# A gated linear attention layer rewritten as four phases over all tokens, with the data between them in DRAM

## The chip, the cores and the metric

The kernel runs on one NeuronCore of one Trainium2 chip. The metric is the device time of one execution in microseconds (us); lower is better. The engines have these names in the profile: PE is TensorE (PEld is its weight load), DVE is VectorE, ACT is ScalarE, POOL is GpSimd, and SP is the engine whose queue issues nearly all DMAs.

## The reference

One layer on 2048 tokens of width 1024, all in float32. Cut to what matters here:

```
u    = rmsnorm(h, ln1_g);  proj = u @ w_in                     # q k v g g_lr cb cc cx
o    = rmsnorm(gla(q, k, v, gate), gn_g) * silu(g)             # gated linear attention, chunked
y    = cb * causal_conv3(cc * cx)
h    = h + concat(o, y) @ w_out                                # "mixing"
u2   = rmsnorm(h, ln2_g);  a, b = split(u2 @ w_gate_upffn)     # 1024 -> 2 x 2816   "up"
h    = h + (silu(a) * b) @ w_down                              # 2816 -> 1024       "down"
u3   = rmsnorm(h, ln3_g);  gate = sigmoid(u3 @ w_ple_gate)
h    = h + gate * (p @ w_ple_proj);  out = rmsnorm(h, lnf_g)   # "embed"
```

## The kernel before

Every float32 operand of a long product is split into a high part (a ScalarE cast to a reduced float32) and a low part (a VectorE subtraction), and each product is made in three passes of matmuls (high by high, high by low, low by high; `unit`, line 139). Splits of weights are made by `split` (lines 99 and 100, tiles `hl`), those of activations by `split_into` (lines 149 and 150).

The 2048 tokens are worked on in four blocks of 512, and one block goes through the whole layer before the next one begins: `mixing`, output projection, up, down, embed. The activations of a block never leave the on-chip memory; the weights are loaded and split again for each block. TensorE executes in the order in which the code emits its work (a manual schedule); the other engines and the DMA queue have an order that a scheduler made at build time, and each executes its own list strictly in that order. Small pieces that depend on other engines (transposes, the attention's small products) are put between long products some "ticks" later; a tick is about a dozen matmuls.

The parts of a block that the change touches:

- **Up.** 22 chunks of 128 hidden columns. The first four are plain products (`up`). The other 18 (`up_fast`) use Winograd's form of Strassen's method: the width of 1024 is halved, the two outputs a and b are the two column halves, and the 512 tokens are halved, so that seven products of 256 columns stand for eight. The four sums of weights are made on GpSimd (line 658, 128 columns each), the sums of token operands once per block in `token_sums` (line 633 and the lines behind it).
- **Down.** Plain: for each set of hidden chunks in `DOWN_SETS`, both halves of the output columns, four token tiles, three matmuls of 512 columns per chunk. Sets of down are interleaved with up chunks, so the hidden activations are consumed soon after they are made. The products are added to `h` on VectorE (line 571).
- **Norms.** `norm_to`: a Square with a sum on ScalarE (line 161), two small GpSimd operations (lines 163 and 165), one scaling on VectorE (line 180), eight transposes on TensorE (line 190), and the split.

The rotating buffers of the DMA'd weights (`raw`, 4 buffers) and of their splits (`hl`, 12 buffers) set how far weights can be prepared ahead.

```
for i, n in enumerate(FIRST_ORDER if c == NPLAIN else ORDER):      # up_fast, per hidden chunk
    o, u, bk, hf = PRODUCTS[n]
    unit(half(bk, hf), lhs(o), rhs(*u), 4, lambda: after_product(n), i % 2 == 1)   # 256 columns
...
for n in range(2):                                                 # down, per set
    wd = weights(w_down, [(n * 512, 512)], c0, nch)
    for ti in range(NT):
        unit(ps, lambda k, s: mT[c0 + k][:, s, tok_of(ti)], wd, nch, d_done)       # 512 columns
```

Of the kernel before, what the change touches and what calls it, by code (L numbers as in the profile page):

```python
# [27 lines left out]
DOWN_SETS = ((0, 4), (4, 4), (8, 4), (12, 4), (16, 6))  # L28
GLA_WAIT = 10
N1, N2, N3 = 7, 3, 3  # L30
NPLAIN = 4
ORDER = (1, 2, 4, 5, 6, 7, 3)
FIRST_ORDER = (1, 2, 3, 4, 5, 6, 7)
# [5 lines left out]
def hybrid_layer(ctx: ExitStack, tc: tile.TileContext,  # L39
# [9 lines left out]
    big = ctx.enter_context(tc.tile_pool(name="big", bufs=4))  # L49
    hlp = ctx.enter_context(tc.tile_pool(name="hlp", bufs=12))  # L50
    rawp = ctx.enter_context(tc.tile_pool(name="rawp", bufs=4))
    w4p = ctx.enter_context(tc.tile_pool(name="w4p", bufs=12))
    t2p = ctx.enter_context(tc.tile_pool(name="t2p", bufs=5))
    tiny = ctx.enter_context(tc.tile_pool(name="tiny", bufs=4))
    ps_mm = ctx.enter_context(tc.tile_pool(name="ps_mm", bufs=4, space=bass.MemoryType.PSUM))
    ps_tr = ctx.enter_context(tc.tile_pool(name="ps_tr", bufs=2, space=bass.MemoryType.PSUM))
    ps_g = ctx.enter_context(tc.tile_pool(name="ps_g", bufs=2, space=bass.MemoryType.PSUM))

    def w4(shape, dt=F32):
        return w4p.tile(shape, dt, name="w4")  # L60

    def t2(shape, dt=F32):
        return t2p.tile(shape, dt, name="t2")

    def mm_bank():
        return ps_mm.tile([P, 512], F32, name="mm")

    def tr_bank():
        return ps_tr.tile([P, 512], F32, name="tr")

    def g_bank():
        return ps_g.tile([P, 512], F32, name="g")
# [11 lines left out]
    nc.gpsimd.memset(mhalf, -0.5)  # L84

# [1 line left out]
    def load_pair(src, k0, width, segs):  # L87
        """rows of the k-chunks k0, k0+1 of the named column segments"""
        raw = rawp.tile([P, 2, width], F32, name="raw")
        o = 0  # L90
        for c, n in segs:
            nc.sync.dma_start(out=raw[:, :, o:o + n],
                              in_=src[k0 * P:(k0 + 2) * P, c:c + n].rearrange("(k p) n -> p k n", p=P))
            o += n
        return raw

    def split(raw, width):
        hl = hlp.tile([P, 2, width], F32R, name="hl")
        nc.scalar.copy(out=hl[:, 0, :], in_=raw)  # L99
        nc.vector.tensor_tensor(out=hl[:, 1, :], in0=raw, in1=hl[:, 0, :].bitcast(F32), op=ALU.subtract)  # L100
        return hl
# [25 lines left out]

    def later(n, fn):
        queue.append((clock[0] + n, fn))
        queue.sort(key=lambda e: e[0])  # L130
# [3 lines left out]
    def unit(out_ap, lhs, rhs, nk, done=None, ticks=True):  # L134
        """out = sum over k of lhs(k).T @ rhs(k), three passes over the split operands"""
        n = out_ap.shape[-1]
        for k in range(nk):
            for i, (a, b) in enumerate(PASSES):
                nc.tensor.matmul(out=out_ap, lhsT=lhs(k, a), rhs=rhs(k, b),  # L139
                                 start=(k == 0 and i == 0), stop=(k == nk - 1 and i == 2))  # L140
            if n > 300 and nk > 6 and k == nk // 2 - 1:
                tick()
        if done is not None:
# [8 lines left out]
    def new_uT():  # L152
        return [big.tile([P, 4, 2, T], F32R, name="uT") for _ in range(2)]
# [3 lines left out]

    def rstd_of(src, dst):
        """per-token 1/rms of the [128, 1024] rows of src; dst is overwritten by the squares"""
# [15 lines left out]
    def norm_to(src, u, ti, gain, delay, eng=nc.vector, xn=None):  # L175
        if xn is None:
            xn = w4([P, D])
        rs = rstd_of(src, xn)
        if eng is nc.vector:
            eng.scalar_tensor_tensor(out=xn, in0=src, scalar=rs, in1=gain, op0=ALU.mult, op1=ALU.mult)  # L180
        else:
            nc.vector.tensor_scalar(out=xn, in0=src, scalar1=rs, scalar2=None, op0=ALU.mult)
            eng.tensor_tensor(out=xn, in0=xn, in1=gain, op=ALU.mult)

        def transposes():
            for kk in range(2):
                tp = tr_bank().rearrange("p (a b) -> p a b", b=P)
                for a in range(4):
                    c = (kk * 4 + a) * P
                    nc.tensor.transpose(out=tp[:, a, :], in_=xn[:, c:c + P], identity=ident)  # L190
                split_into(u[kk][:, :, 0, ti * P:(ti + 1) * P], u[kk][:, :, 1, ti * P:(ti + 1) * P], tp)
        if delay is None:
            return transposes
        later(delay, transposes)
# [9 lines left out]
    # remaining constants  # L204
    gng = const.tile([P, 1], F32, name="gng")
    bg = const.tile([P, 2], F32, name="bg")
    cw = const.tile([P, 3, 4], F32, name="cw")
    wgu = const.tile([P, 256], F32, name="wgu")
    lrT = const.tile([P, T], F32, name="lrT")
    smask = const.tile([P, T], F32, name="smask")  # L210
    state = const.tile([P, 2, 256], F32, name="state")
    halo = const.tile([P, 4, 2], F32, name="halo")
    s_sb = {g: const.tile([P, 4, P], F32, name=f"s_sb{g[0]}{g[1]}") for g in GROUPS}
    masks = {L: const.tile([P, 4, P], U8, name=f"mask{L}") for L in LEVELS[2:] + (2,)}

    nc.gpsimd.memset(lrT, 0.0)
    nc.gpsimd.memset(wgu, 0.0)

    def fill_constants():
        after(nc.gpsimd.dma_start(out=wgu[0:16, :], in_=w_gate_up), last["rs"])  # L220
        after(nc.gpsimd.dma_start(out=bg, in_=b_gate.rearrange("(j p) -> p j", p=P), allow_slow_non_contiguous=True), last["rs"])
        after(nc.gpsimd.memset(smask, 1.0), last["rs"])
        nc.gpsimd.memset(smask.rearrange("p (c t) -> p c t", t=P)[:, :, 0:1], 0.0)
        after(nc.gpsimd.dma_start(out=gng, in_=gn_g[0].rearrange("(p o) -> p o", o=1)), last["rs"])
        for i in range(3):
            after(nc.gpsimd.dma_start(out=cw[:, i, :], in_=conv_w[i].rearrange("(j p) -> p j", p=P),
                                      allow_slow_non_contiguous=True), last["rs"])
        after(nc.gpsimd.memset(state, 0.0), last["rs"])
        after(nc.gpsimd.memset(halo, 0.0), last["rs"])
        for t in s_sb.values():  # L230
            after(nc.gpsimd.memset(t, 0.0), last["rs"])

    def fill_mask(L):
        """one where the column's token takes from the row's token at this level"""
        m = masks[L]
        f = t2([P, P])
        after(nc.gpsimd.memset(f, 1.0), last["rs"])
# [616 lines left out]
```

## Time and profile before

| | |
|---|---|
| time, median of 3 runs | 2568.82 us (2568.5 to 2569.72) |
| span of the profiled execution | 2568.4 us |
| PE busy | 2519.0 us (98%) |
| DVE busy | 1706.5 us (66%) |
| ACT busy | 1087.8 us (42%) |
| POOL busy | 918.6 us (36%) |
| DMA | 265.18 MB, mean 103 GB/s |
| mean granted TensorE clock | 0.996 |

The profile is of one execution, whose span is 0.4 us under the median of the times. "Busy" counts the time in which an engine has an instruction in work. A group row reads: line, engine, operation, what is written from what, the shape, the count, then busy time and mean duration in ns of one, then the idle time before it and what ended it. A timeline row reads: start, duration, the merged instructions and their count, and in brackets the idle time before and what ended it. The duration of a TensorE row has a modelled tail, so rates are taken from start to start.

### The profile page before, as it was taken

What the parts mean: (1) busy time and instruction counts of PE and PEld (TensorE: products, weight loads), DVE (VectorE), ACT (ScalarE), POOL (GpSimd) and SP (SyncE); (2) the same over time, 40 slices, a digit from 0 to 9 for tenths busy, and PEclk for the clock granted to TensorE, in tenths of its full rate; (3) what the DMA queues carried; (4) which work ended last, traced back from release to release, by engine and by line L of the source; (5) the groups of instructions that cost most, each with busy time, mean ns of one, the idle gap of its engine ahead of it and who ended that gap; (6) DMA issues with size and microseconds to landing.
All of it is one profiled execution on the core that took longest, in us unless ns stands there. A gap on an engine that the chain in (4) does not pass through costs nothing.

```text
span 2568.4 us, 42117 instructions
## 1 busy us (share of the span) xinstructions
PE 2519.0 (98%) x15616; PEld 2196.1 (86%) x15616; DVE 1706.5 (66%) x2628; ACT 1087.8 (42%) x2104; POOL 918.6 (36%) x1468
## 2 busy tenths in 40 slices
PE   7999999999999999999999999999999999999998
PEld 6778899998878889999887888999878788899987
DVE  4665777776475567777647566777765756677774
ACT  4433444444443344444543343444454334344442
POOL 3301366631130246663121024666313102466620
PEclk9999999999999999999999999999999999999999
DMA  4224233344322333334333223333433232233341
GB/s 157 66 66 132 83 99 99 103 128 149 107 85 69 111 91 99 99 99 154 127 99 99 98 67 91 103 103 99 156 124 108 81 107 72 85 105 102 102 151 52
DMA packets 268686, 265.18 MB, mean 103 GB/s; under 512 B 20656, under 2 KB 202944, under 8 KB 268480
## 3 DMA queue, kind: packets, MB, share of 16 engines
q1 hardware_dynamic: 268288, 262.47, 32.7%
q8 instruction: 122, 2.00, 0.3%
q14 instruction: 84, 0.69, 0.1%
q0 software_dynamic: 192, 0.02, 0.0%
HBM read 254.04 MB, written 8.39 MB: 102 GB/s over the span
## 4 chain that ended last, share of the span: by engine, by line
PE 85%; issue 7%; DVE 4%; POOL 2%; ACT 2%; DMA 0%; SPq 0%; DVEq 0%; POOLq 0%; ACTq 0%
PE mm L139 67%; PE g L139 12%; PE g L330 1%; PE tr L190 1%; DVE uT L150 1%; DVE hl L100 1%; PE g L418 1%; PE g L423 1%; DVE w L281 1%; DVE w L633 1%; POOL rs L165 0%; POOL uT L303 0%; POOL uT L302 0%; PE g L427 0%; PE g L320 0%
## 5 line engine op out<-in xcount | busy, mean ns | idle before, releaser
L139 PE MATMUL mm<-uT,hl 128*128 128x256 f32 (+1 forms) x6528 | 1098.8, 325 | 23.4 <-DVE hl L100 21.8
L139 PEld LDWEIGHTS mm<-uT,hl 128*128 128x128 f32 x6528 | 942.7, 190 | 133.7 <-DVE hl L100 29.6
L100 DVE TENSOR_TENSOR hl<-raw,hl 128x512 fp32r<-128x512 f32 (+2 forms) x1152 | 804.7, 734 | 146.6 <-ACT hl L99 145.1
L99 ACT CAST hl<-raw 128x512 fp32r<-128x512 f32 (+2 forms) x1152 | 634.0, 593 | 618.8 <-PE mm L139 408.7
L658 POOL TENSOR_TENSOR raw<-raw 128x128 f32<-128x128 f32 x1152 | 700.7, 634 | 490.4 <-DMA raw<-in_w_gate_upffn_dram 390.8
L139 PE MATMUL mm<-hl,w 128*128 128x512 f32 x2304 | 542.5, 394 | 0.1
L139 PEld LDWEIGHTS mm<-hl,w 128*128 128x128 f32 x2304 | 430.4, 188 | 100.2 <-ACT w L698 1.8
L139 PE MATMUL mm<-hl,uT 128*128 128x512 f32 (+1 forms) x2256 | 458.0, 361 | 3.4 <-DVE uT L150 2.1
L139 PEld LDWEIGHTS mm<-hl,uT 128*128 128x128 f32 x2256 | 374.8, 188 | 69.1 <-DVE uT L150 2.7
L139 PE MATMUL g<-uT,hl 128*128 128x256 f32 x2592 | 331.4, 282 | 0.0
L139 PEld LDWEIGHTS g<-uT,hl 128*128 128x128 f32 x2592 | 319.6, 189 | 1.7
L571 DVE TENSOR_TENSOR w<-mm,w 128x512 f32<-128x512 f32 x192 | 131.9, 687 | 221.0 <-PE mm L139 200.8
L163 POOL TENSOR_SCALAR ms<-ss 128x1 f32<-128x1 f32 x64 | 19.5, 304 | 652.5 <-ACT w L161 462.9
L149 ACT CAST uT<-tr 128x512 fp32r<-128x512 f32 x96 | 54.0, 583 | 68.8 <-PE tr L190 68.7
L678 DVE TENSOR_TENSOR w<-mm,t 128x256 f32<-128x256 f32 (+1 forms) x144 | 79.3, 553 | 2.3
L698 ACT CAST w<-w 128x512 fp32r<-128x512 f32 x72 | 44.8, 622 | 82.4 <-DVE w L697 82.4
L161 ACT ACTIVATE w<-w 128x1024 f32<-128x1024 f32 x48 | 51.0, 1062 | 56.3 <-DVE w L571 24.0
L150 DVE TENSOR_TENSOR uT<-tr,uT 128x512 fp32r<-128x512 f32 x96 | 63.8, 685 | 10.0 <-ACT uT L149 9.7
L442 POOL TENSOR_SCALAR ms<-ss 128x4 f32<-128x4 f32 x16 | 3.1, 193 | 188.1 <-ACT t L439 188.1
L697 DVE TENSOR_TENSOR w<-w 128x512 f32<-128x512 f32 x72 | 60.1, 835 | 8.3 <-ACT w L696 8.3
L180 DVE SCALAR_TENSOR_TENSOR w<-w,rs,w 128x1024 f32<-128x1024 f32 x32 | 41.1, 1284 | 34.1 <-POOL rs L165 28.8
L149 ACT CAST uT<-w 128x512 fp32r<-128x512 f32 (+1 forms) x32 | 26.8, 837 | 81.7 <-DVE w L554 61.0
(138 smaller groups left out, 1496.4 us busy)
## 6 DMA issues: line engine op xcount, KB each, us to landing
raw<-in_w_gate_upffn_dram SPq DMA_DIRECT2D x576, 128.0 KB, 2.3
raw<-in_w_down_dram SPq DMA_DIRECT2D x88, 512.0 KB, 3.7
raw<-in_w_in_dram SPq DMA_DIRECT2D x64, 512.0 KB, 4.5
w<-in_x_dram SPq DMA_DIRECT2D x32, 512.0 KB, 6.8
raw<-in_w_in_dram SPq DMA_DIRECT2D x64, 256.0 KB, 4.1
raw<-in_w_out_dram SPq DMA_DIRECT2D x32, 512.0 KB, 4.7
raw<-in_w_gate_upffn_dram SPq DMA_DIRECT2D x64, 256.0 KB, 4.1
raw<-in_w_ple_gate_dram SPq DMA_DIRECT2D x32, 512.0 KB, 4.9
```

What stands on the lines that cost most here:

```text
L99: nc.scalar.copy(out=hl[:, 0, :], in_=raw)
L100: nc.vector.tensor_tensor(out=hl[:, 1, :], in0=raw, in1=hl[:, 0, :].bitcast(F32), op=ALU.subtract)
L139: nc.tensor.matmul(out=out_ap, lhsT=lhs(k, a), rhs=rhs(k, b), start=(k == 0 and i == 0), stop=(k == nk - 1 and i == 2))
L149: nc.scalar.copy(out=hi, in_=src)
L150: nc.vector.tensor_tensor(out=lo, in0=src, in1=hi.bitcast(F32), op=ALU.subtract)
L161: nc.scalar.activation(out=dst, in_=src, func=AF.Square, scale=1.0 / 32.0, accum_out=ss)
L180: eng.scalar_tensor_tensor(out=xn, in0=src, scalar=rs, in1=gain, op0=ALU.mult, op1=ALU.mult)
L571: last["h"] = nc.vector.tensor_tensor(out=hs, in0=ps, in1=hs, op=ALU.add)
L658: op = lambda e, o, x, y, f: e.tensor_tensor(out=raw[:, o, :], in0=raw[:, x, :], in1=raw[:, y, :], op=f)
L678: add = lambda out, x, y: nc.vector.tensor_tensor(out=out, in0=x, in1=y, op=ALU.add)
L697: MENG.tensor_tensor(out=af[:, 0:T], in0=af[:, 0:T], in1=af[:, T:2 * T], op=ALU.mult)
L698: nc.scalar.copy(out=m[:, 0, :], in_=af[:, 0:T])
```

## The change

The layer is now made in four phases, each over all 2048 tokens, one after the other, with DRAM tensors between them:

1. **Mixing**, in four blocks of 512 tokens as before, up to the output projection and the second norm. The residual stream goes to DRAM (`h_mid`), and so do the transposed normed tokens: `norm_to_ops` writes them as the seven token operands of the up products (`up_ops`). The operands that are sums of two tokens 512 apart are made on GpSimd for every second block and written by four more DMAs for each token tile.
2. **Up**, on two halves of 1024 tokens, all 22 chunks in the form of seven products, each now of 512 columns. Weights are loaded and split twice in all in place of four times. The seven operands are loaded and split at the start of each half. The hidden activations go to DRAM.
3. **Down**, on two halves of 1024 tokens. 18 of the 22 chunks, in three sets of two times three, are made with seven products in place of eight (halves of the hidden width, the output columns and the tokens); the last four are plain. Each set needs eight GpSimd sums of 128 by 1536, and 14 splits of that size.
4. **Embed**, with both halves of the gate's and the projection's weights kept on chip for all blocks.

`hl` has 11 buffers, `raw` 4; each phase opens its own pools, and their memory lies over that of the phase before. The core of the diff, new functions shortened:

```diff
-DOWN_SETS = ((0, 4), (4, 4), (8, 4), (12, 4), (16, 6))
+BT = 2 * T
+DOWN_SETS = ((0, 3), (6, 3), (12, 3))
+DOWN_LAST = 18
...
+    def norm_to_ops(src, tile, ops, gain, delay):
+        xn = normed(src, gain)
+        def transposes():
...
+            for kk in range(2):
+                nc.scalar.copy(out=ut[:, kk], in_=transposed(xn, kk))
+            if tile < NT:
+                put(1, ut[:, 0]); put(2, ut[:, 1]); return
+            put(3, ut[:, 1])
+            tensor(g, s[:, 0], ut[:, 0], old[:, 0], ALU.subtract)
+            put(5, s[:, 0])
+            tensor(g, s[:, 1], ut[:, 1], s[:, 0], ALU.subtract)
+            put(6, s[:, 1])
...
+    def up_phase(st):
+        for b in range(NBB):
+            for c in range(NHC):
+                w = up_weights(c)
+                if c == 0:
+                    for n in UP_ORDER:                       # (1, 6, 2, 5, 7, 3, 4)
+                        U[n] = pl["U"].tile([P, 4, 2, T], F32R, name="U")
+                        for i in range(2):
+                            raw = pl["raw"].tile([P, 2, T], F32, name="raw")
+                            nc.sync.dma_start(out=raw, in_=up_ops[b][n][:, 2 * i:2 * i + 2, :])
+                            split_into(U[n][:, 2 * i:2 * i + 2, 0, :], U[n][:, 2 * i:2 * i + 2, 1, :], raw)
...
+                    product(bk[n], w(OPERAND[n]), lambda k, s: U[n][:, k, s, :], 4, start=on is None, ...)
...
+    def down_phase(st):
+            for si, (c0, nk) in enumerate(DOWN_SETS):
+                a11, r11 = raw_w(c0, nk, 0), raw_m(c0, nk, 0)
+                if si == 0:
+                    for t in range(2 * NT): ...              # eight loads of h, 512 KB each
+                a21, a22 = raw_w(c0, nk, 1), raw_w(c0 + nk, nk, 1)
+                r12, r22 = raw_m(c0, nk, 1), raw_m(c0 + nk, nk, 1)
+                W[1], M[1] = halves("wh", a11, nk), halves("mh", r11, nk)
+                sub(a11, a11, a21)                           # GpSimd, 128 x 1536
+                tensor(G, cols(a21), cols(a21), cols(a22), ALU.add)
+                sub(s2, a22, a11); sub(r11, r12, r11); sub(r12, r22, r12); sub(t2_, r22, r11)
+                go(1, None, keep)
+                W[6], M[6] = halves("wh", s2, nk), halves("mh", t2_, nk)
+                go(6, None, ...)                             # then 2, 5, 7, 3, 4; 36 matmuls each
```

What moves is seen best in the lists that the engines execute. The first place is the seam from mixing to up, on the DMA queue (SP). Before, behind the last weights of the output projection (`w_out`) come the weights of up and nothing else:

```order
L92 DMA raw_1842<-in_w_out_dram 128x2x512
L92 DMA raw_1850<-in_w_out_dram 128x2x512
...
L92 DMA raw_2036<-in_w_gate_upffn_dram 128x2x256 x2
L92 DMA raw_2045<-in_w_gate_upffn_dram 128x2x256 x2
L92 DMA raw_2054<-in_w_gate_upffn_dram 128x2x256 x2
```

Now (`up0_6` and `up0_2` are the second and third token operands that the up phase needs, `up1_*` those of the later half, which are still being written; `w4_7918`, `w4_7919` and `w4_7935` hold the sums of the last token tile):

```order
L699 DMA raw_8029<-up0_6_107 128x1024
L229 DMA up1_5_113<-w4_7935 512x1x128
L229 DMA up1_6_114<-w4_7935 512x1x128
L229 DMA up1_7_115<-w4_7918 512x1x128
L229 DMA up1_4_112<-w4_7919 512x1x128
L699 DMA raw_8034<-up0_2_103 128x1024
L699 DMA raw_8038<-up0_2_103 128x1024
L699 DMA raw_8043<-up0_5_106 128x1024
```

The loads of five of the seven operands stand behind the four writes of the last token tile, which wait for GpSimd. The second place is the seam from up to down. On the DMA queue, the first weights and activations of the first set (`wr_14943`, `mr_14945`), eight tiles of the residual stream (`h`), and then the rest of the set:

```order
L748 DMA mr_14945<-hid0_2_118 128x512
L773 DMA h_14949<-h_mid0_70 128x1024
...
L773 DMA h_14963<-h_mid7_77 128x1024
L753 DMA wr_14965<-in_w_down_dram 128x3x512
L753 DMA wr_14967<-in_w_down_dram 128x3x512
```

and on GpSimd, the six sums before the set's second product, then two that come later in the set:

```order
L212 TENSOR_TENSOR wr_14943<-wr_14943,wr_14965 128x1536
L212 TENSOR_TENSOR wr_14965<-wr_14965,wr_14967 128x1536
L212 TENSOR_TENSOR wr_14985<-wr_14967,wr_14943 128x1536
L212 TENSOR_TENSOR mr_14945<-mr_14969,mr_14945 128x1536
L212 TENSOR_TENSOR mr_14969<-mr_14973,mr_14969 128x1536
L212 TENSOR_TENSOR mr_14989<-mr_14973,mr_14945 128x1536
L212 TENSOR_TENSOR wr_14985<-wr_15085,wr_14985 128x1536
```

Before, GpSimd had only pieces of 128 columns there, and the weights of down were loaded plainly between those of up:

```order
L658 TENSOR_TENSOR raw_2633<-raw_2633 128x128 x4
L658 TENSOR_TENSOR raw_2646<-raw_2646 128x128 x4
L658 TENSOR_TENSOR raw_2659<-raw_2659 128x128 x4
L658 TENSOR_TENSOR raw_2672<-raw_2672 128x128 x4
L658 TENSOR_TENSOR raw_2932<-raw_2932 128x128 x4
```

The second product of the first set takes the split of `mr_14989`, the sixth of these sums; the third place is TensorE itself, where nothing of another stage stands between the last up product, the first down product (`wh_14977`, `mh_14980`) and the second (`wh_15035`, `mh_15038`):

```order
L142 MATMUL mm_14865<-U_11542,hl_14800 128x512 x3
L142 MATMUL mm_14991<-wh_14977,mh_14980 128x512 x9
L142 MATMUL mm_14992<-wh_14977,mh_14980 128x512 x9
L142 MATMUL mm_14993<-wh_14977,mh_14980 128x512 x9
L142 MATMUL mm_14994<-wh_14977,mh_14980 128x512 x9
L142 MATMUL mm_15041<-wh_15035,mh_15038 128x512 x9
```

In the kernel before, products of up and of down alternate there, chunk by chunk.

More of the change, by code (lines that the diff above doesn't have):

```diff
@@ L214, in hybrid_layer @@
[L214 to L231, printed above, removed]
@@ L316, in level_products @@
                     for a in range(4):
                         for par in range(2):
[L318 to L326 removed]
+                            r, c = head(tp, par, a)
@@ L327, in level_products, with pair_products @@
+            def pair_products(E, K2, tp):
+                sp = [g_bank().rearrange("p (a t) -> p a t", t=P) for _ in range(2)]
                 for a in range(4):
@@ L614, in down, with block @@
+        def block(b, u1, first):
+            mix = mixing(b, u1, first)
+            g2 = gain_tile(ln2_g[0], last["cb"])
+            h = [load_x(b, ti, nc.sync, last["cb"]) for ti in range(NT)]
+            more = b + 1 < NB
+            if more:
+                g1 = gain_tile(ln1_g[0], last["cb"])
+                u1 = new_uT()
+            for n in range(2):
+                wo = weights(w_out, [(n * 512, 512)])
                 for ti in range(NT):
                     ps = mm_bank()
-                    def d_done():
-                        add_to_h(ps, ti, n)
-                        if final and n == 1:
-                            norm_to(h[ti], *final, ti)
@@ new lines, in mixing_phase, with up_weights @@
+        for b in range(NB):
+            u1 = block(b, u1, start if b == 0 else None)
+        flush()
+    w_up_h = w_up.rearrange("(h q p) n -> p q h n", h=2, q=4)
+    OPERAND = {1: 0, 2: 1, 3: 6, 4: 2, 5: 3, 6: 4, 7: 5}
+    def up_weights(c):
+        tiles = []
+        for q in range(4):
+            raw = pl["raw"].tile([P, 8, P], F32, name="raw")
+            nc.sync.dma_start(out=raw[:, 1:3, :], in_=w_up_h[:, q, :, c * P:(c + 1) * P])
+            nc.sync.dma_start(out=raw[:, 0:4:3, :], in_=w_up_h[:, q, :, HID + c * P:HID + (c + 1) * P])
+            op = lambda o, x, y, f: tensor(nc.gpsimd, raw[:, o, :], raw[:, x, :], raw[:, y, :], f)
+            op(6, 1, 0, ALU.subtract)
+            op(4, 0, 3, ALU.add)
+            op(5, 3, 6, ALU.subtract)
+            op(7, 2, 5, ALU.subtract)
+            tiles.append((split(raw[:, 1:5, :].rearrange("p a n -> p (a n)"), 512),
+                          split(raw[:, 5:8, :].rearrange("p a n -> p (a n)"), 384)))
+        return lambda o: (lambda q, s: tiles[q][o // 4][:, s, (o % 4) * P:(o % 4 + 1) * P])
@@ L743, in p_transposes @@
                 tp = tr_bank()
                 for k in range(2):
-                    nc.tensor.transpose(out=tp[:, k * P:(k + 1) * P], in_=pt[:, k * P:(k + 1) * P],
-                                        identity=ident)
-                for k in range(2):
-                    tok = tok_of(ti)
-                    split_into(pT[k][:, 0, tok], pT[k][:, 1, tok], tp[:, k * P:(k + 1) * P])
-            later(5 + ti // 2, p_transposes)
-        lnf = gain_tile(lnf_g, gate)
-        more = b + 1 < NB
```

1123 lines of the change are left out of this document (583 added, 540 removed).

## The prediction

> **What bounds the kernel now.** I read the page's engine table and its chain first: if one engine is the whole path, the change is worth its difference on that engine plus what the new seams add.
>
> ```profile
> span 2568.4 us, 42117 instructions
> PE 2519.0 (98%) x15616; PEld 2196.1 (86%) x15616; DVE 1706.5 (66%) x2628; ACT 1087.8 (42%) x2104; POOL 918.6 (36%) x1468
> PE 85%; issue 7%; DVE 4%; POOL 2%; ACT 2%; DMA 0%; SPq 0%; DVEq 0%; POOLq 0%; ACTq 0%
> ```
>
> TensorE is busy for 98% and makes 85% of the chain. So next comes its timeline, for the price of a matmul (start of a row to start of the next) and for idle times.
>
> ```profile
> 194.54 33.58 PE L139 MATMUL mm<-hl,uT 128*128 128x512 f32 x144
> 227.96 1.04 PE L190 MATMUL tr<-ident,w 128*128 128x128 f32 x8
> ...
> 312.95 22.26 PE L139 MATMUL mm<-hl,w 128*128 128x512 f32 x96
> 335.04 3.03 PE L139 MATMUL g<-uT,hl 128*128 128x256 f32 x24
> 272.19 20.86 PE L139 MATMUL mm<-uT,hl 128*128 128x512 f32 x82 [3.36 <-DVE hl L100]
> 906.98 20.73 PE L139 MATMUL mm<-uT,hl 128*128 128x512 f32 x82 [2.65 <-DVE hl L100]
> 1541.48 20.74 PE L139 MATMUL mm<-uT,hl 128*128 128x512 f32 x82 [2.85 <-DVE hl L100]
> 2176.59 20.86 PE L139 MATMUL mm<-uT,hl 128*128 128x512 f32 x82 [2.70 <-DVE hl L100]
> 639.67 0.63 PE L190 MATMUL tr<-ident,w 128*128 128x128 f32 x4 [1.06 <-DVE uT L150]
> ```
>
> 144 matmuls of 512 columns take 33.42 us, 0.2321 each; in down 96 take 22.09, 0.2301 each. The rows with 82 are the plain chunks inside up, one in each block: TensorE waits 11.6 us in all there, for weight splits. The windows (length, busy of PE, PEld, DVE, ACT, POOL, clock, DMA share, GB/s) give the 256-column rate, the clock behind such a wait and the DMA's rate:
>
> ```profile
> 335.04:437.05 102.01, 102.01 (x769) 97.83 (x768) 82.72 (x134) 48.10 (x94) 65.77 (x101) 1.00 0.38 113
> 272.00:276.00 4.00, 3.81 (x11) 3.04 (x12) 4.00 (x8) 0.54 (x2) 0.00 (x0) 0.65 0.40 111
> 276.00:280.00 4.00, 4.00 (x18) 3.19 (x17) 0.08 (x1) 0.60 (x1) 3.75 (x9) 0.92 0.55 152
> 10.00:14.00 4.00, 3.28 (x12) 2.63 (x13) 3.06 (x6) 3.21 (x7) 0.00 (x0) 1.00 1.07 397
> ```
>
> In the up stretch a run of 84 seven-product matmuls comes every 10.00 us, 0.1190 each. After a stall the clock is 0.65 for 4 us and 0.92 for the next 4: 1.4 + 0.3 = 1.7 us lost beyond the idle time itself. DMAs move 397 GB/s when they have the chance.
>
> **Gains on TensorE.** Up: before, a block has 1704 matmuls of 256 columns (1512 of the 18 fast chunks, 192 of plain ones) and 96 of 512: 1704 × 0.1190 + 96 × 0.2321 = 225.1; four blocks 900.2. After: 2 halves × 22 chunks × 84 = 3696 of 512 columns, 857.9. Gain 42.4. Down: 4 × 528 = 2112 at 0.2301 = 486.0; after, 2 × (3 sets × 252 + 192) = 1896, 436.3. Gain 49.7. The four stalls at the plain chunks and the slow clock behind each: 11.6 + 4 × 1.7 = 18.4. In sum 110.5. Mixing's and embed's products and all transposes stay as many as they were, so I cost their matmuls at nothing.
>
> **The prices of the other engines**, by groups of one shape (count | busy, mean ns | idle and who ended it), two lines' own views (least/median/most ns) and the DMA list (count, size, us to landing):
>
> ```profile
> L100 DVE TENSOR_TENSOR hl<-raw,hl 128x512 fp32r<-128x512 f32 x832 | 604.9, 751 | 130.3 <-ACT hl L99 129.0
> L150 DVE TENSOR_TENSOR uT<-w,uT 128x1024 fp32r<-128x1024 f32 x16 | 19.2, 1219 | 0.0
> L150 DVE TENSOR_TENSOR uT<-w,uT 128x512 fp32r<-128x512 f32 x16 | 11.0, 690 | 0.3
> L149 ACT CAST uT<-w 128x1024 fp32r<-128x1024 f32 x16 | 16.9, 1054 | 20.7 <-DVE w L637 16.7 <-DVE w L639 2.9 <-DVE w L638 1.1
> L99 ACT CAST hl<-raw 128x512 fp32r<-128x512 f32 x832 | 489.6, 620 | 567.4 <-PE mm L139 403.9 <-POOL raw L658 114.3 <-issue 37.3
> L571 DVE TENSOR_TENSOR w<-mm,w 128x512 f32<-128x512 f32 x192 | 131.9, 687 | 221.0 <-PE mm L139 200.8 <-DMA w<-in_x_dram 19.9
> L280 POOL TENSOR_TENSOR uT<-uT 128x512 f32<-128x512 f32 x8 | 10.1, 1289 | 125.7 <-ACT uT L278 125.7
> L378 POOL TENSOR_TENSOR w<-w 128x1024 f32<-128x1024 f32 x4 | 8.3, 2071 | 0.0
> L633 POOL TENSOR_TENSOR w<-uT 128x1024 f32<-128x1024 f32 x8 | 22.9, 2889 | 0.0
> L161 ACT ACTIVATE w<-w 128x1024 f32<-128x1024 f32 x48 | 51.0, 1062 | 56.3 <-DVE w L571 24.0 <-DVE w L774 15.5 <-DMA w<-in_x_dram 11.3
> L165 POOL TENSOR_TENSOR rs<-ms,mhalf 128x1 f32<-128x1 f32 x64 | 37.6, 588 | 5.3
> L180 DVE SCALAR_TENSOR_TENSOR w<-w,rs,w 128x1024 f32<-128x1024 f32 x32 | 41.1, 1284 | 34.1 <-POOL rs L165 28.8 <-ACT hl L99 5.3
> L658 POOL TENSOR_TENSOR raw<-raw x1152: 448/464/2582, 248.4 to 2452.9; 128x128 f32<-128x128 f32 x192
> L633 DVE TENSOR_TENSOR w<-uT x8: 1211/1578/2641, 254.6 to 2164.1; 128x1024 f32<-128x1024 f32 x8
> raw<-in_w_in_dram SPq DMA_DIRECT2D x64, 512.0 KB, 4.5
> raw<-in_w_down_dram SPq DMA_DIRECT2D x88, 512.0 KB, 3.7
> ```
>
> No row has 1536 columns. ScalarE's cast goes by 0.62 and 1.05 to 1.49 us, VectorE's split by 0.69 and 1.22 to 1.74. For a GpSimd sum, 0.45 (least) at 128 and 1.29 at 512 columns give 3.52; through 512 and 2.07 at 1024 it is 2.85, through 2.89 it is 4.33. I take 3.52, the middle. By these, a down set (252 matmuls, 58 us) needs 14 × 1.74 + 28 × 0.69 = 44 on VectorE, 28 on GpSimd, 21 on ScalarE: all hidden in the steady state. If that cover is gone, rival 1 says what it costs.
>
> **The seams.** Here TensorE has no other stage's products to run.
>
> A, mixing to up. Five operands' loads stand on SP behind the last tile's four writes, and those behind the tile's chain: add 0.69, square 1.06, the two small GpSimd steps about 0.9, scaling 1.28, transposes 1.04, two copies 1.2, four sums 5.16: 11.3; with ten hand-overs at about 0.5 and four issues, 18.3 (an estimate). Landing 4.1 (between 3.7 and 4.5), cast and split 2.3: 24.7. Then the other half and four further operands at two splits each, 2.44: 35.7, and the last product 2.8: 38.5, against 19.5 for chunk 0 without waits. 19.0, and 3 for chunk 1's weights, queued behind the operands: 22. Least 16, if the hand-overs are nearly free; most 30, if GpSimd is also late with the tile before.
>
> B, the second half of up: operands can only be loaded as their raw buffers come free: 6 (2 to 12; the ends are one and five operands late at 2.44).
>
> C, up to down. SP issues the first set's hidden loads about 2.2 after the last product; 0.79 MB of them, 4.19 MB of `h` and 0.79 MB of weights stand ahead of the first sum's second operand: 14.5 at 397 GB/s, about 19.0 with latency. Six sums: 21.1, so 40.1; cast and split 3.2, hand-overs 0.8: 44.1. In that time TensorE has one product, 36 × 0.230 = 8.3. Idle 35.8, slow clock 1.7: 37.5. By the sum's bounds 33 to 42, and if `h` loads share the queues unevenly 29 to 46.
>
> D, down's second half: GpSimd's sums wait for the in-place split of the first operand, and behind three of them (10.6) stand the small norm steps of the last tile: 9 (0 to 18; nothing, if the scheduler's other work covers it, or twice).
>
> E, down to embed: the last tile's chain without sums, 6.5; write and load 4.1; four splits 4.9; then 20 weight splits at 0.75, 15; hand-overs and the last product about 4: 34.5 until a tile's 60 matmuls (13.9) are through. 20.6 (14 to 28; from half of the weight splits early, to the write's landing paid once more).
>
> F, embed's three block borders: a transpose waits for a bank about 3.2 now, against 1.06: 6.4 (1 to 9).
>
> G, one `hl` buffer less in mixing: 3 (0 to 8, from a split of 0.75 late four or ten times).
>
> Costs: 22 + 6 + 37.5 + 9 + 20.6 + 6.4 + 3 = 104.5 (62 to 151 if all ends came together; half-widths added as squares give 18). The sum: 2568.4 − 110.5 + 104.5 = 2562.4, and with the 0.4 by which the median lies above the span, **2563**; own range 2545 to 2581. A large change on TensorE, eaten by three seams.
>
> **Rivals.** 1, slower: VectorE and GpSimd take turns. L633's rows on VectorE go from 1.21 to 2.64, beside GpSimd's of 2.9, and L658's on GpSimd from 0.45 to 2.58: each sometimes waits out the other. Then a half's 18 GpSimd sums (63.4), 42 splits (73.1) and 84 adds (57.7) stand in one row: 194 against 174.6 for the three sets' 756 matmuls × 0.231, 19.6 a half, 39 in all: 2602. It decides when less than a third of the adds run beside GpSimd (194 − 20 = 174); against it, the adds read a bank of products, not two tiles, and L571 shows 0.69 on the mean. The Trainium skill, "SBUF — State Buffer", section "SBUF: two separate sides", has this as a rule: a VectorE operation with two on-chip-memory inputs and a GpSimd operation that reads the memory lock each other out wholly. By it the splits would take turns with the sums and the adds would not, 137 of 175 us, and the time stays at the forecast; the two rows' maxima agree with it.
>
> 2, faster: the scheduler's lists are only orders; if loads land ahead and the sums run as soon as two operands are there, A, C and E halve: 40 less, 2523. For it: DMAs have most of their rate free (113 of 397 GB/s). Against: each list is in order, and the writes stand ahead.
>
> 3, the change does not do what it says: products of 512 columns are no faster per column (0.238, twice 0.119), and up gains 20.6 in place of 42.4: 2585. Against: the x144 row.
>
> **How the numbers follow.** The forecast 0.52, rival 1 0.18, rival 2 0.18, rival 3 0.06, something else 0.06. The range 2530 to 2601 reaches to most of 2 and up to 1. About 0.2% (5.1 us: 2563.7 to 2573.9) is what a measurement can tell from no change. The forecast's 0.52 divides into 0.26 faster, 0.14 same, 0.12 slower; with rivals and rest (half each way): faster 0.47, same 0.14, slower 0.39.
>
> **What would show it.** Up's matmuls at 0.232 and 857.9 in sum, with no idle time between chunks; down's sets at 58 us each. Idle times on TensorE of about 20 (A, spread over five operands), 36 behind the first down product (C, ended by VectorE's split after GpSimd), 20 at the first embed tile (E, ended by weight splits). I am wrong if a sum of 1536 lasts beyond 4.3, if down's sets last over 60, or if C is under 29.

## The result: 3.3% slower

The changed kernel takes 2653.26 us (median of 4 runs, 2651.32 to 2654.65), the kernel before 2569.27 us in the same session: ratio 1.0326, 95% interval 1.0311 to 1.0340. The forecast was 2563 us. The profiled execution has a span of 2652.8 us, 84.4 more than before. Its page begins:

```profile
span 2652.8 us, 32365 instructions
PE 2466.7 (93%) x11896; PEld 1995.2 (75%) x11896; DVE 1461.9 (55%) x1916; ACT 923.3 (35%) x1565; POOL 852.8 (32%) x1116
PE 54%; issue 14%; POOL 6%; DMA 3%; DVE 3%; ACT 2%; SPq 0%; POOLq 0%; DVEq 0%; ACTq 0%
```

TensorE is busy for 52.3 us less than before, not for the 92.1 less that the matmuls are worth, so 39.8 us of it went to slower matmuls; and it is idle for 186.1 us in place of 49.4, 136.7 more. 136.7 − 52.3 = 84.4. The slower matmuls go with the granted clock: taken in windows of 4 us, TensorE's busy time times the share of the clock that was not granted is 51.9 us here and 7.9 in the kernel before (an estimate). VectorE and GpSimd have less work than before, and still TensorE waits. Where it waits is read from its timeline (start, duration, instructions, in brackets the idle time before and who ended it):

```profile
928.39 1.04 PE L197 MATMUL tr<-ident,w 128*128 128x128 f32 x8
...
938.65 1.94 PE L197 MATMUL tr<-ident,w 128*128 128x128 f32 x8 [9.22 <-DVE w L190]
942.21 0.79 PE L142 MATMUL mm<-U,hl 128*128 128x512 f32 x1 [1.62 <-ACT U L156]
961.83 0.79 PE L142 MATMUL mm<-U,hl 128*128 128x512 f32 x1 [12.74 <-ACT U L156]
...
992.45 411.48 PE L142 MATMUL mm<-U,hl 128*128 128x512 f32 x1766 [1.21 <-ACT hl L99]
1405.32 6.42 PE L142 MATMUL mm<-U,hl 128*128 128x512 f32 x25 [1.39 <-DVE hl L100]
...
1854.63 1.22 PE L142 MATMUL mm<-wh,mh 128*128 128x512 f32 x2 [10.00 <-ACT mh L156]
1856.42 10.28 PE L142 MATMUL mm<-wh,mh 128*128 128x512 f32 x34 [0.57 <-DVE mh L157]
1891.49 1.22 PE L142 MATMUL mm<-wh,mh 128*128 128x512 f32 x2 [24.79 <-ACT mh L156]
1895.01 58.78 PE L142 MATMUL mm<-wh,mh 128*128 128x512 f32 x250 [2.30 <-DVE mh L157]
1956.69 3.89 PE L142 MATMUL mm<-wh,mh 128*128 128x512 f32 x9 [2.90 <-DVE h L212]
...
2020.04 2.28 PE L142 MATMUL mm<-wh,mh 128*128 128x512 f32 x9 [2.91 <-DVE h L212]
...
2146.11 1.97 PE L197 MATMUL mm<-ident,w 128*128 128x128 f32 x8 [12.01 <-DVE w L190]
```

The up phase in between is as forecast: 411.48 us without a gap, 0.233 us a matmul. The seams are not. (The first half of up ends at 1401.2, after 1848 matmuls; the last 11 of this row and the next one, at 1405.32, already belong to the second half.) In the table each is the stretch between two marks of this timeline less its matmuls at full rate, and mixing is what remains of the 84.4:

| | forecast | measured |
|---|---|---|
| A, mixing to up (928.4 to 1401.2, less 22 chunks and 8 transposes) | 22 | 43.1 |
| B, second half of up (to 1844.6) | 6 | 14.5 |
| C, up to down (to 1953.8, less 288 matmuls) | 37.5 | 42.9 |
| D, rest of down: its second half, and waits at the borders of its sets | 9 and 0 | 43.7 |
| E, down to embed | 20.6 | 26.5 |
| F, embed's borders | 6.4 | 16.1 |
| G, mixing (remainder) | 3 | 8.1 |
| sum | 104.5 | 194.9 |

C's idle time is 37.7 us, near the 35.8 of the forecast; the rest goes with a slower clock. GpSimd's part of C is a row of six sums that starts when their operands have landed:

```profile
1866.48 10.29 POOL L212 TENSOR_TENSOR wr<-wr 128x1536 f32<-128x1536 f32 x3 [53.92 <-DMA wr<-in_w_down_dram]
1876.72 13.21 POOL L212 TENSOR_TENSOR mr<-mr 128x1536 f32<-128x1536 f32 x3
```

D is the largest miss. The 12.01 us at 2146.11 are the wait that the forecast had there (9). Beside it stands a kind of wait that the forecast does not have at all: at each border of two sets inside a half product 6 waits for additions to `h` (18.9 us idle in eight waits, two at each border). What VectorE, ScalarE and GpSimd do there, from their timeline:

```profile
1940.53 3.52 DVE L157 TENSOR_TENSOR wh<-wr,wh 128x1536 fp32r<-128x1536 f32 x1 [4.31 <-ACT wh L156]
...
1950.83 3.50 POOL L212 TENSOR_TENSOR wr<-wr 128x1536 f32<-128x1536 f32 x1
1950.91 1.48 ACT L156 CAST mh<-mr 128x1536 fp32r<-128x1536 f32 x1 [10.41 <-POOL mr L212]
...
1952.42 3.52 DVE L157 TENSOR_TENSOR mh<-mr,mh 128x1536 fp32r<-128x1536 f32 x1 [6.58 <-ACT mh L156]
...
1955.87 0.68 DVE L212 TENSOR_TENSOR h<-mm,h 128x512 f32<-128x512 f32 x1
1956.03 3.48 POOL L212 TENSOR_TENSOR mr<-mr 128x1536 f32<-128x1536 f32 x1 [1.70 <-DVE mh L157]
...
1956.47 4.64 DVE L157 TENSOR_TENSOR wh<-wr,wh 128x1536 fp32r<-128x1536 f32 x1
...
1961.04 1.87 DVE L212 TENSOR_TENSOR h<-mm,h 128x512 f32<-128x512 f32 x3
```

A GpSimd sum of 1536 columns lasts 3.5 us in the median, as estimated, and 3.9 on the mean. But a VectorE split that comes while one runs does not end before it: 3.52 and 4.64 us in place of 1.74. The split at 1952.42 ends 1.6 us after the sum that began at 1950.83 and ended at 1954.33; the next sum begins only behind that split. So it is throughout down: of the 25 splits that overlap a sum, 23 last 3.47 to 5.03 us; none of the others lasts over 2.07. Additions are not held up: 26 of them lie wholly within a sum, and each lasts 0.67 to 0.69 us.

The addition at 1955.87 is late for two reasons, both in VectorE's list, where the split of 1952.42 stands ahead of it. That split needs the last of the row of six sums, which takes 24.0 us from 1926.91 on: ScalarE's cast waits 10.41 us for it, and VectorE itself stands idle for 6.58 us. Then the split is blocked. Product 6 needs the bank that the addition reads.

### The profile page after: what moved, and what is told of

Its sections match the earlier page's. It is cut to its first block, busy times and chain, and to the rows that moved or that the text cites. A ratio compares the mean times of both kernels' runs of the same rounds, so it can differ in the third digit from the quotient of the medians.

```text
span 2652.8 us, 32365 instructions
## 1 busy us (share of the span) xinstructions
PE 2466.7 (93%) x11896; PEld 1995.2 (75%) x11896; DVE 1461.9 (55%) x1916; ACT 923.3 (35%) x1565; POOL 852.8 (32%) x1116
## 4 chain that ended last, share of the span: by engine, by line
PE 54%; issue 14%; POOL 6%; DMA 3%; DVE 3%; ACT 2%; SPq 0%; POOLq 0%; DVEq 0%; ACTq 0%
PE mm L142 51%; POOL mr L212 2%; DMA raw<-up 1%; POOL wr L212 1%; DVE wh L157 1%; POOL w L212 1%; PE g L385 1%; POOL raw L212 1%; DMA w<-up 1%; ACT mh L156 1%; DMA mr<-hid 1%; POOL rs L177 0%; DMA h<-h_mid 0%; DVE hl L100 0%; DMA raw<-in_w_gate_upffn_dram 0%
## 5 line engine op out<-in xcount | busy, mean ns | idle before, releaser
L142 PE MATMUL mm<-U,hl 128*128 128x512 f32 x3696 | 873.9, 398 | 30.1 <-ACT U L156 15.3
L142 PEld LDWEIGHTS mm<-U,hl 128*128 128x128 f32 x3696 | 700.7, 190 | 203.4 <-ACT U L156 17.3
L212 POOL TENSOR_TENSOR raw<-raw 128x128 f32<-128x128 f32 x704 | 395.2, 589 | 498.1 <-DMA raw<-in_w_gate_upffn_dram 442.3
L142 PE MATMUL mm<-wh,mh 128*128 128x512 f32 x1896 | 452.5, 400 | 57.9 <-ACT mh L156 34.8
L142 PE MATMUL mm<-uT,hl 128*128 128x512 f32 x1920 | 480.4, 404 | 9.6 <-DVE hl L100 5.5
L99 ACT CAST hl<-raw 128x512 fp32r<-128x512 f32 (+1 forms) x628 | 357.5, 590 | 376.9 <-PE mm L142 263.5
L100 DVE TENSOR_TENSOR hl<-raw,hl 128x512 fp32r<-128x512 f32 (+1 forms) x628 | 432.6, 717 | 78.9 <-ACT hl L99 78.5
L142 PEld LDWEIGHTS mm<-wh,mh 128*128 128x128 f32 x1896 | 364.5, 194 | 140.3 <-ACT mh L156 35.6
L142 PEld LDWEIGHTS mm<-uT,hl 128*128 128x128 f32 x1920 | 357.9, 191 | 101.9 <-DVE hl L100 11.0
L142 PE MATMUL mm<-hl,u 128*128 128x512 f32 x768 | 188.1, 402 | 2.5 <-ACT hl L99 1.8
```

The source lines that it names most:

```text
L212: return e.tensor_tensor(out=out, in0=a, in1=b, op=op)
```

## The experiments

Times of this section are medians, to be set against 2653.26 us; ratios are to the kernel before, run beside each.

**The order of the products (d_order).**

```diff
+                W[2], M[2] = halves("wh", a12, nk), halves("mh", r21, nk)     # moved up, with its loads
+                go(2, 1, lambda t, x: add(h[t][:, lo], x))
                 W[6], M[6] = halves("wh", s2, nk), halves("mh", t2_, nk)
                 go(6, None, lambda t, x: add(acc[t], x))
```

> Down's products in the order 1, 2, 6, 5, 7, 3, 4 in place of 1, 6, 2, 5, 7, 3, 4; nothing else. My theory: the waits at the borders of the sets (18.9 us of idle time ended by VectorE's adds, some 23 with the slow clock) come from product 6 taking the banks of the set's last product, whose adds stand behind splits; with product 2 in between they have 16.6 us in place of 8.3. So these go, and the seam into down changes little, since the operands of product 2 are loaded last: 2625 to 2635 against 2653. Rival: VectorE is simply late by its share of the work, and the wait moves to another product: 2645 to 2655.

2661.41 us, ratio 1.0356 (1.0341 to 1.0372): slower than either range. The wait moved, as the rival says, and grew. Its timeline at the same border:

```profile
1960.85 4.18 PE L142 MATMUL mm<-wh,mh 128*128 128x512 f32 x9 [5.90 <-ACT wh L156]
```

Product 2's weights are split late now: in the lists of ScalarE and VectorE they stand behind the split that waits for GpSimd's sums. Giving one wait more room does not help while these lists wait.

**The loads of the residual stream (d_hlate).**

```diff
                 a11, r11 = raw_w(c0, nk, 0), raw_m(c0, nk, 0)
-                if si == 0:  ...                         # eight loads of h
                 a21, a22 = raw_w(c0, nk, 1), raw_w(c0 + nk, nk, 1)
                 r12, r22 = raw_m(c0, nk, 1), raw_m(c0 + nk, nk, 1)
+                if si == 0:  ...
```

> The eight loads of the residual stream are issued behind the loads of the first set's weights and activations, not ahead of them. My theory: these 4.19 MB (10.6 us at 397 GB/s) stand ahead of the first sum's second operand in the first half of down, so the wait for product 6 gets some 10 us shorter: 2641 to 2645. Rival: the sums themselves bound it, since GpSimd waits for other operands anyway: 2650 to 2654.

2658.81 us, ratio 1.0345 (1.0329 to 1.0361): nothing gained. The mechanism of the first theory is there, and most of its gain is given back in the following products:

```profile
1881.94 1.22 PE L142 MATMUL mm<-wh,mh 128*128 128x512 f32 x2 [13.28 <-ACT mh L156]
1885.46 10.57 PE L142 MATMUL mm<-wh,mh 128*128 128x512 f32 x35 [2.30 <-DVE mh L157]
1898.25 0.50 PE L142 MATMUL mm<-wh,mh 128*128 128x512 f32 x1 [2.22 <-DVE wh L157]
1901.59 51.57 PE L142 MATMUL mm<-wh,mh 128*128 128x512 f32 x214 [2.83 <-DVE mh L157]
```

The wait for product 6 falls from 24.79 to 13.28 us, and 252 matmuls from there then take 71.2 us (1881.94 to 1953.15) in place of 62.3 (1891.49 to 1953.79): two new waits of 2.2 and 2.8, and slow matmuls, 0.30 us each in the second row. From the last up product to the end of the first set it takes 106.1 us in place of 109.2; the rest of what is missing here lies outside this seam, as up already ends 2.4 us later in this execution.

**Four sums first (d_sums4).**

```diff
-                tensor(G, cols(a21), cols(a21), cols(a22), ALU.add)     # both now behind go(6)
-                sub(r12, r22, r12)
```

> GpSimd makes only the four sums that product 6 needs ahead of it; the other two come behind. My theory: product 6 of the first set waits for a row of six sums at 3.5 us and their lock waits, so 7 to 8 us go there, once or twice: 2638 to 2647. Rival: the two late sums then hold up product 5 or the splits, and the time stays: 2650 to 2655, or more.

2640.11 us, ratio 1.0277 (1.0260 to 1.0294): 13 us, more than one wait gives. The wait for product 6 at C falls from 24.79 to 20.25 us, and the waits at the set borders shrink from 18.9 to 9.9 us in all, though GpSimd makes as many sums as before: the length of the row ahead of the split counts there.

**Writes on GpSimd's queue (a_gw).**

```diff
+            put = lambda n, t: nc.gpsimd.dma_start(out=ops[n][:, :, tok], in_=t)   # operands 5, 6, 7, 4
```

> The four writes of the token sums go out on GpSimd's own DMA queue, not on SP. My theory: at the seam into up the operand loads were held on SP behind writes that waited for GpSimd (issued 30 us after the last output projection product); without these they issue some 17 us sooner: 2632 to 2640. Rival: the memory of the operand tiles is not free before the last tile's work ends, or issuing on GpSimd delays its sums: 2648 to 2656.

2655.84 us, ratio 1.0337 (1.0321 to 1.0352). The rival holds. The idle time only changes its places:

```profile
932.28 1.59 PE L197 MATMUL tr<-ident,w 128*128 128x128 f32 x8 [3.97 <-DVE w L190]
942.73 1.94 PE L197 MATMUL tr<-ident,w 128*128 128x128 f32 x8 [8.86 <-DVE w L190]
...
928.45 0.75 POOL L237 DMA_DIRECT2D up<-w  x1
...
931.34 0.74 POOL L237 DMA_DIRECT2D up<-w  x1 [0.30 <-POOL w L212]
```

Each write now takes GpSimd some 0.75 us to issue, and the norm steps of the next token tile, which are on GpSimd too, come later.

**All sums of down on VectorE (d_vall).**

```diff
-                sub = lambda out, x, y: tensor(G, cols(out), cols(x), cols(y), ALU.subtract)
+                sub = lambda out, x, y: tensor(V, cols(out), cols(x), cols(y), ALU.subtract)
```

(and the one addition alike)

> All eight sums of a down set are made on VectorE, none on GpSimd. My theory (the two engines lock each other out): a split of 1536 columns then lasts 1.74 us throughout in place of 2.28 on the mean, a sum 1.74 in place of 3.9, and GpSimd's small norm steps stand behind nothing. Product 6 of the first set comes some 10 us sooner, the 12 us at the half's border go, the waits at the set borders shrink although VectorE now has about 58 us of work in a set of 58: 2618 to 2633 against 2653. Rival (no lock, VectorE was late by its share of work): VectorE becomes the bound and the sets get longer: 2655 to 2680.

2594.69 us, ratio 1.0092 (1.0075 to 1.0109): 58.6 us gained, where 20 to 35 were expected. The views of line 157 (splits: least, median, longest ns) and of line 212 (sums), first of the changed kernel, then of this one:

```profile
L157 DVE TENSOR_TENSOR wh<-wr,wh x50: 1215/1748/4968, 1847.6 to 2331.7; 128x1536 fp32r<-128x1536 f32 x42, 128x1024 fp32r<-128x1024 f32 x8
L212 POOL TENSOR_TENSOR wr<-wr x24: 3414/3510/5020, 1866.5 to 2272.4; 128x1536 f32<-128x1536 f32 x24
```

```profile
L157 DVE TENSOR_TENSOR wh<-wr,wh x50: 1215/1750/2068, 1846.4 to 2271.9; 128x1536 fp32r<-128x1536 f32 x42, 128x1024 fp32r<-128x1024 f32 x8
L212 DVE TENSOR_TENSOR wr<-wr x24: 1747/1750/1758, 1865.0 to 2222.7; 128x1536 f32<-128x1536 f32 x24
```

None of these splits is longer than 2.07 us now, and a sum takes half of its time on GpSimd. TensorE, on the page and in the timeline:

```profile
PE 2448.6 (94%) x11896; PEld 1983.6 (77%) x11896; DVE 1479.9 (57%) x1964; ACT 924.3 (36%) x1565; POOL 662.1 (26%) x1068
...
1878.64 1.22 PE L142 MATMUL mm<-wh,mh 128*128 128x512 f32 x2 [13.60 <-ACT mh L156]
1882.15 178.61 PE L142 MATMUL mm<-wh,mh 128*128 128x512 f32 x778 [2.28 <-DVE mh L157]
```

From the first product 6 on there is one run of 778 matmuls, 0.2296 us each, through all set borders of the first half. In the second set VectorE is busy for 54.2 of 57.1 us there, and in the changed kernel for 50.0 of 63.4, blocked time included. It has more to do, and TensorE no longer waits for it: its share of work alone was not the bound. By stage, the seam C (from the last up product to the end of the first set) falls from 109.2 to 97.8 us, and the rest of down by 47.1, all of the 43.7 that D cost.

**The token sums of mixing on VectorE (a_v).**

```diff
-            g = nc.gpsimd
+            g = nc.vector
```

> The token sums of the mixing phase are made on VectorE, 0.69 us each in place of 1.29 on GpSimd; their writes stay on SP. My theory: GpSimd is then free for the norm steps and the writes on SP wait less, so the operand loads are issued some 10 us sooner: 2638 to 2645. Rival: the chain is bound by the read-back of the older tile's operands and the in-order queue, not by the sums: 2649 to 2655.

2641.70 us, ratio 1.0275 (1.0259 to 1.0290): 11.6 us, as expected, but only in part where it was expected. The wait for the last transposes falls from 9.22 to 5.56 us, and the operand loads are issued 11 us sooner. But 5.1 of these are there because mixing as a whole ends sooner (its last product at 923.26 in place of 928.39), and the long wait moves into the first up product:

```profile
947.43 20.37 SPq L699 DMA_DIRECT2D raw<-up  x10
...
947.46 4.69 PE L142 MATMUL mm<-U,hl 128*128 128x512 f32 x11 [13.25 <-DVE U L157]
```

The sums on VectorE now wait for the read-back of the older operands there (6.37 and 4.80 us), and the split that this product needs stands behind them in VectorE's list. From the last product of mixing to the end of the first up chunk it takes 53.6 us in place of 56.2.

What remains there is the queue; in the changed kernel's timeline SP's list at this place reads:

```profile
942.92 6.17 SPq L229 DMA_DIRECT2D up<-w  x4
949.18 1.28 SPq L226 DMA_DIRECT2D w<-up  x2
...
953.77 4.29 SPq L229 DMA_DIRECT2D up<-w  x4
958.16 17.81 SPq L699 DMA_DIRECT2D raw<-up  x10
```

The last tile's read-back of the older operands (949.18) stands behind the four writes of the tile before, which wait for its sums, and the operand loads stand behind the last tile's writes.

**Embed's transposes off the borders (e_p).**

```diff
+                    if pT is None:                # first block: behind the first gate product
+                        pT = p_tokens(b)
...
+                if ti == 1 and b + 1 < NB:
+                    nextp = p_tokens(b + 1)
```

> Embed: the transposes of p for the next block stand in the middle of a block, not at its border, and for the first block behind the first gate product, so that the gate's weights are loaded ahead of p. My theory: the borders' waits (8.4, 8.1 and 2.8 us) go, and of the 27 us at the phase's start some 8 (its wait for the load of p): 2624 to 2632. Rival: the start is bound by the loads of 7 MB of weights and tokens in any order, and only the borders are gained: 2633 to 2640.

2644.71 us, ratio 1.0284 (1.0269 to 1.0299): 8.6 us, a smaller gain than either range has. Most of it is in the borders, whose waits go. At the phase's start the wait is still there, only under another name, as the rival has it:

```profile
2401.46 7.51 PE L142 MATMUL mm<-hl,u 128*128 128x512 f32 x24 [13.01 <-ACT hl L99]
```

**TensorE kept busy (warm).**

```diff
+                    for _ in range(3):            # ahead of product 6 in the first up chunk
+                        product(warm, w(OPERAND[1]), lambda k, s: U[1][:, k, s, :], 4)
...
+                    for t in range(11):           # ahead of product 6 in the first down set
+                        product(warm, lambda k, s: M[1][:, k, s, tok_of(t % 4)], lambda k, s: W[1][:, k, s, :], nk)
```

> TensorE runs 36 matmuls whose result nobody uses ahead of product 6 in the first up chunk, and 99 ahead of product 6 in the first down set, in the time in which it is idle. My theory: the low granted clock behind these waits (0.5 to 0.68 for 28 us in up, 0.57 in down) is caused by the idle time, and filling it gives back some 6 to 10 us: 2643 to 2648. Rival: the matmuls there are slow because their operands come late, and the clock costs nothing by itself: 2651 to 2655.

2654.87 us, ratio 1.0323 (1.0308 to 1.0339): no gain. The windows (length, busy of PE, PEld, DVE, ACT, POOL, clock, DMA share, GB/s) of the same stretches, the changed kernel first:

```profile
942.00:962.00 20.00, 6.03 (x13) 3.97 (x13) 4.20 (x3) 2.37 (x4) 11.44 (x8) 0.50 0.79 230
1867.00:1892.00 25.00, 0.51 (x1) 0.50 (x2) 8.89 (x3) 5.20 (x5) 24.84 (x7) 0.59 0.36 134
1892.00:1900.00 8.00, 5.70 (x16) 4.00 (x15) 8.00 (x3) 4.93 (x4) 6.26 (x2) 0.57 0.59 180
```

```profile
942.00:962.00 20.00, 13.94 (x48) 10.53 (x48) 2.35 (x2) 0.94 (x2) 11.03 (x8) 0.84 0.74 214
1867.00:1892.00 25.00, 23.48 (x104) 19.12 (x102) 8.52 (x2) 4.41 (x4) 24.78 (x7) 1.00 0.44 163
1892.00:1900.00 8.00, 4.74 (x11) 3.42 (x12) 7.46 (x3) 6.00 (x5) 6.31 (x2) 0.57 0.47 126
```

In down the clock is full where TensorE is filled (in up it is 0.84 in place of 0.50), and it is 0.57 right behind, with two waits of 2.07 and 2.71 us: the extra products end a little before the operands come, and product 6 then waits for its halves as before. So the experiment shows that the clock is higher where the idle time is filled, but does not price it, since short waits stay behind the long one. In up, a new wait of 8.36 us came up, ended by an addition; the extra products take a bank there, which may be why.

**Only the first sets on VectorE (d_v0).**

```diff
+                SE = V if si == 0 else G                     # for all eight sums
```

> Only the sums of the first set of each half are on VectorE, those of the other two stay on GpSimd. My theory: the seam into down and the border of the halves (together some 27 us) are mended, the waits at the set borders inside a half (some 20) stay, since the sums there still meet the splits: 2622 to 2632. Rival: the set borders come from something else than the sums, and what is left here over the kernel with all sums on VectorE (2594.7) is under 15: 2600 to 2610.

2625.71 us, ratio 1.0216 (1.0202 to 1.0230): 27.6 us gained, 31.0 short of all sums on VectorE. The total is as expected. The wait for product 6 at C falls from 24.79 to 13.52 us, that at the half's border goes, and at each border of sets inside a half the wait for an addition stays:

```profile
2011.70 2.32 PE L142 MATMUL mm<-wh,mh 128*128 128x512 f32 x9 [2.96 <-DVE h L212]
```

**No sums in down (nosum).** The products take unsummed operands, so this times the kernel without these 48 sums.

```diff
-                sub(a11, a11, a21)          # and the seven others
```

> Leaves out all GpSimd sums of down (the products take operands that are not summed, so the result is another one). My theory: the sums cost through the lock, and VectorE carries them at nearly no cost in the steady state; so this is faster than the kernel with all sums on VectorE (2594.7) only by the sums that stand ahead of product 6, some 8 to 10 us: 2582 to 2590. Rival: VectorE is full with the sums and costs time in every set: 2565 to 2578.

2587.54 us, ratio 1.0069 (1.0054 to 1.0085): 65.7 us under the changed kernel, and only 7.2 under the one with all sums on VectorE. That is in the expected range. On GpSimd the sums cost 65.7 us; on VectorE, which had less time to spare, 7.2.

**What is worth keeping, together (best2, best3).** best2 is d_vall, a_v, e_p, d_sums4 and d_hlate in one; best3 adds:

```diff
+        if tile >= NT:                                # ahead of the norm, no longer behind its transposes
+            old = w4([P, 2, 4, P]); ...
...
-        pools(st, {"wp": 20, "pr": 4,
+        pools(st, {"pr": 4, "wp": 20,
+                wg.append(weights(w_pg, [(0, 512)]))  # ahead of the first block's tokens
```

> Together: all token and down sums on VectorE, four of the six first sums ahead of product 6, the residual stream's loads behind the first set's operands, and p's transposes off the borders of embed. My theory: with GpSimd out of the way the order of loads and sums counts, which it did not while the two engines took turns, and the seam into down loses a further 10 to 14 us beside the single gains (58.6 + 11.5 + 8.5): 2560 to 2567, a little faster than the kernel before (2569). Rival: what is gained at the seam is given back in the next products, as with the loads alone: 2572 to 2580.

2569.43 us against 2570.52, ratio 0.9998 (0.9989 to 1.0006): no difference from the kernel before, 2 us above the expected range. d_vall's 2594.69 less the gains of a_v and e_p would be 2574.5, so the order of sums and loads at C is worth 5 us together, not 10 to 14. The traces say the same: the seam C takes 92.9 us here and 97.8 with all sums on VectorE.

> The kernel before it, and in addition: the older tile's operands are read back before the norm of the younger one, and the first half of the gate's weights is loaded while down's last products run, into memory that is free by then. My theory: the two seams with waits for transfers (13 us each on TensorE) lose about half: 2546 to 2556. Rival: the queue is in order and the loads come where they came before: 2558 to 2566.

2556.29 us, ratio 0.9946 (0.9933 to 0.9958): 0.5% faster than the kernel before, the fastest here, and 0.3 us above the expected range. Its page and the three seams:

```profile
PE 2445.2 (96%) x11896; PEld 1981.5 (78%) x11896; DVE 1494.4 (58%) x1996; ACT 922.8 (36%) x1565; POOL 620.4 (24%) x1036
...
946.10 0.80 PE L142 MATMUL mm<-U,hl 128*128 128x512 f32 x1 [5.92 <-ACT U L156]
1852.92 0.73 PE L142 MATMUL mm<-wh,mh 128*128 128x512 f32 x2 [2.05 <-ACT mh L156]
2312.86 8.89 PE L142 MATMUL mm<-hl,u 128*128 128x512 f32 x24 [7.77 <-ACT u L156]
```

The waits of 12.7 (A), 24.8 (C) and 13.0 us (E, in the kernel with e_p alone) are 5.9, 2.1 and 7.8; at C two new ones of 3.89 and 2.69 us follow. TensorE is still idle for 110.0 us (2555.2 − 2445.2), more than twice as long as in the kernel before.

## Why the prediction was wrong

**The gains were right.** Up runs at 0.233 us a matmul of 512 columns, down at 0.2296 where nothing blocks it. Rival 3 is out.

**The failed step is "all hidden in the steady state".** It compared busy times in a set (44 us on VectorE and 28 on GpSimd against 58 on TensorE) as if the two engines ran side by side; where it let splits and sums take turns, it put all additions beside the sums (137 of 175 us). So it put the set borders at nothing. The runs show sets of 65.2 and 63.4 us (from one product 6 to the next: 1891.49, 1956.69, 2020.04). In the second of them splits and sums take turns, and of 19.0 us of additions only 5.1 run beside a sum. VectorE or GpSimd is at work in 63.0 of its 63.4 us.

The Trainium skill, "SBUF — State Buffer", section "SBUF: two separate sides", says that a VectorE operation with two inputs in on-chip memory and a GpSimd operation that reads this memory block each other for the whole instruction; the traces agree (3.47 to 5.03 us for splits beside a sum, 1.75 in the median). The prediction used that rule, and drew from it that the time stays at the forecast: it counted what the blocked instructions cost, and not what is queued behind them, nor that most additions would come when no sum runs.

By d_vall, the placing of the sums is 58.6 us of the 84 lost: 11.4 at C, the rest at the set borders and the half's border, where the small norm steps stand behind three sums. By d_v0 a border keeps its waits as long as the sums of the set behind it are on GpSimd. That sums on GpSimd cost this is shown, and that VectorE's own share of work does not (d_vall). How the waits divide is not shown: the two engines together have too little room, and the additions stand in VectorE's list behind a split that waits for a row of six sums and is then blocked. The two hang together, because the lists decide how many additions run beside sums. d_sums4 fits both: its row ahead of the split is shorter, 7.3 us of additions run beside sums in its second set, and that set lasts 61.4 us. d_vall takes away the blocking and the long sums at once, and no run keeps one without the other.

**Rival 1, that the engines take turns, was nearer than the forecast.** Its condition, less than a third of the additions beside GpSimd, was met (5.1 of 19.0 us). Its sum counts 18 GpSimd sums of 1536 columns in a half, and there are 24. With 24 it is 215 us against 174.6, 40.7 a half, 81 in all, and its time 2644. That this is near the measured 2653 would be luck: the three sets of the two halves took 190.4 and 186.9 us, 28 more than forecast in all, and the rest of the loss lies elsewhere.

**C's idle time was right (35.8 forecast, 37.7 measured), and so were its two parts, loads and then sums.** The first sum begins 21.9 us after the last up product, when its operand has landed (19.0 forecast), and six sums take 23.4 (21.1 forecast). From the last up product to the end of the first set it takes 109.2 us; taking 10 us off the loads gives 106.1 (d_hlate), two sums less 106.4 (d_sums4), all sums on VectorE 97.8, and all of this together 92.9 (best2). Neither part alone is worth much, because the products behind take most of it back.

**A was half of what it is (22 against 43.1).** The chain was read as one tile's. It is two tiles' on one queue: the read-back of older operands, which the forecast left out, waits behind the writes of the tile before, and on GpSimd the norm steps of the last tile wait behind the sums of the one before. The operand loads go out 29.8 us after the last output projection product (958.16 − 928.39), not 18.3. The hand-overs between engines were not it: those from the last tile's addition to its transposes took 0.03 to 0.15 us where the chain is not held up, not 0.5. The read-back moved ahead in best3 bears this out: from the last mixing product to the end of the first up chunk it takes 46.8 us there, 52.4 in best2, 56.2 in the changed kernel. Sums on VectorE alone (a_v) gave 2.5 at this place.

**B was 14.5 us, not 6, and above its range (2 to 12).** From 1404 to 1436 TensorE stands idle for 8.4 us in eleven short waits, for splits of operands and of weights, and the clock is 0.78 between 1420 and 1440. No run takes this apart.

**The clock was left out behind the new waits.** It was charged once, 1.7 us at C. TensorE's busy time says 39.8 us in all. No run here prices it alone; d_vall has 18.1 us less busy time on TensorE than the changed kernel (2466.7 and 2448.6) with the same matmuls, so it goes with the waits.

**E and F were short by 6 and 10 us.** In F the transposes of p wait for a split and for a load at each block border, where the forecast had one wait for a bank, and the matmuls behind are slow. In E they wait 8.5 us for the load of p at the phase's start. G, a remainder of 8.1 us against 3, was taken apart by no run. Rival 2, that the seams are covered, is out: the waits are in the timeline.

## What to carry to other kernels

Before work goes to GpSimd as "free", look at what VectorE does beside it. Here splits, whose two inputs are both in on-chip memory, took turns with the sums, and additions, which read one input from a bank of products, did not have to. So add up in one row what takes turns, and with it whatever the lists will not place beside a sum: here most additions, since they stand in VectorE's list behind splits that are blocked or wait for GpSimd. The busy times of each engine by itself do not show that; the longest against the median duration of the same instruction (4.97 against 1.75 us here) does. And a phase border costs a chain through every ordered queue that feeds it: write down the last items of each queue, the read-backs and the writes that wait among them, before a price is put on it.

## What was not expected of the hardware

Moving 48 sums from a less used engine (GpSimd, 32% busy) to a more used one (VectorE, 55%) gained 58.6 us; leaving them out altogether would gain only 7.2 more. And waits of 2 to 3 us can be enough for a low granted clock: it is 0.57 in the 8 us around two of them (2.07 and 2.71 us), right behind 25 us at full clock. But the length of a wait does not settle it: the nine matmuls behind the 2.90 us before 1956.69 ran at 0.61, those behind the 2.91 us before 2020.04 at 1.00.
